# A second buffer for the split probabilities (ph) in a two-layer hybrid attention / mLSTM backbone

## The chip, the cores and the metric

The kernel runs on one core of one Trainium2 chip. The metric is device time in microseconds (us) of one execution, taken as the median of several runs. One core has TensorE (PE in the profile, with its weight loads as PEld), VectorE (DVE), ScalarE (ACT), GpSimd (POOL) and SyncE (SP), which issues the DMAs. Each engine works its own instructions off in the order in which they were emitted and waits on semaphores for the others.

## The reference

A latent stream x of 2048 tokens and a context of 256 tokens, both 1024 wide, go through two layers. In each layer the normed and modulated input is projected; the columns are split into windowed attention (8 query heads, 2 key/value heads of 64) and a bidirectional mLSTM (4 heads of 128); both are gated, concatenated and projected out. Cut to what the change touches, the attention is:

```python
s_win = jnp.einsum('bnqhgd,bnkhd->bhgnqk', qb, kw) * scale      # 128 queries, 3 x 128 keys
s_ctx = jnp.einsum('bnqhgd,bchd->bhgnqc', qb, kc) * scale       # 256 context keys
s_sink = sink.reshape(1, KV, G, 1, 1, 1)                        # one logit per head
p = jax.nn.softmax(jnp.concatenate([s_win, s_ctx, s_sink], axis=-1), axis=-1)
out = einsum(p_win, vw) + einsum(p_ctx, vc)
x = x + gate_x * (jnp.concatenate([att_x * silu(az), m_x], -1) @ w_out)
```

The context rows only attend to the context, and they go through the out-projection in the first layer alone.

## The kernel before

All matrix products of float32 values are made from pairs of fp16 parts (hi, lo) in three passes, so an operand is scaled by a power of two and split before it goes to TensorE.

**Attention.** It runs in four units of two heads in a layer. A unit goes over blocks of 128 queries (18 in the first layer, 16 in the second). For a block b and each of its heads h, `score` takes one of the two 1024-wide PSUM tiles `d` and multiplies query and key pairs into it: 640 columns for an inner block (two neighbours, two context blocks, the block itself), 512 or 256 elsewhere. Its `post` task then does, in this order: VectorE adds the mask and takes the maximum; VectorE makes the bias (`smx`); ScalarE takes the exponent in place, with the row sum; ScalarE copies the result times 16384 into the left half of the fp16 tile `ph` (line 1108); VectorE writes the rest, product minus that copy, to the right half (line 1110), after which `d` is given back; SyncE issues a DMA transpose of `ph` into one of three tiles `pp` (line 1114), and when that has read it, `ph` is free again. `ph` has one buffer (line 388). Once both heads' transposes have landed, `pv` multiplies probabilities and values ("PV", `b<-vp,pp` in the profile, 20 matmuls for an inner block). Around these, `qproj` (q for two blocks, `b<-xt,wa`, 24 matmuls of 256 columns) and `zproj` (the gate, `b<-wa,xt`, 24 of 128 columns) project with the weights `wa`. There are 136 blocks in all, hence 272 scores and transposes and 136 PVs.

**mLSTM.** For each of four heads `mproj` projects q, k and v and runs the forward states, and `mmix` goes over the chunks of 128 tokens backwards: a load of decay rows (`mb<-mD`, three buffers), GpSimd and ScalarE make the decay from them, TensorE makes two transposed products (`kT`), the projections of the output gates (`b<-woz,xt`, 24 matmuls of 256 columns) and five float32 products with states and values (`b<-V,p`, `b<-V,toz`, `b<-s,mb`), and VectorE, ScalarE and GpSimd norm and gate the result, which goes to DRAM (`mixD`).

**Out-projection.** For a block, `loader` fetches its row of `mixD`, VectorE takes the maximum (`held<-g`), ScalarE and VectorE split it (`xt`), SyncE transposes the pair, and only after that issues the next block's load. TensorE then does 48 matmuls of 512 columns (`b<-xt,xt` in the second layer). It needs `w_out`, which is loaded into the room of the layer's input, once the attention and the mLSTM of a token group have both read that for the last time.

**What sets the order.** The program isn't written in the order in which it runs. The attention stream (`alpha`, weight 308), the mLSTM stream (`beta`, weight 560) and some smaller ones are generators. A planner (`Plan.run_until`) keeps an estimated clock for each engine and an estimated time at which each tile is written and read; `till` holds a generator until its operand is there by that estimate, `get` until a buffer is free by it, and the streams of like priority take turns by the share of TensorE's time that they have had. The next piece is emitted from whatever can go on. An instruction's place on its engine therefore follows from the estimates: a buffer that the planner holds to be taken moves all that stands behind it, and lets other streams go ahead. For the DMA transpose of `ph` the estimate is fixed by its size:

```python
            if name == "dma_start_transpose":
                return 0.8, 2.2 + b / 300e3
```

Nearly every instruction is emitted through one helper, so the profile shows line 179 for all of them, and work is told apart by the tiles' names.

Of the kernel before, what the change touches and what calls it, by code (L numbers as in the profile page):

```python
# [7 lines left out]
F16 = mybir.dt.float16  # L8
# [5 lines left out]
P = 128  # L14
D = 1024
# [49 lines left out]
def _span(v):  # L65
    """Name and range of the bytes of one partition (or of DRAM) that v covers."""
    dims = list(v.ap)
    size = 2 if v.dtype == F16 else 4
    off = v.offset
    if v.space != bass.MemoryType.DRAM:  # L70
        step = dims[0][0]
        off = off % step if step else off
        dims = dims[1:]
    lo = hi = off
    for st, n in dims:
        if st < 0:
            lo += st * (n - 1)
        else:
            hi += st * (n - 1)
    return v.name, lo * size, (hi + 1) * size  # L80
# [6 lines left out]
class Plan:  # L87
    """The order of emission.  Streams and tasks are generators: they yield True after a piece of work,
    a time to wait for, or None while a flag or a buffer is missing.  The engines' times are estimated."""

# [10 lines left out]

# [1 line left out]
    def _times(self, table, v):  # L103
# [76 lines left out]

# [1 line left out]
    def buffers(self, tag, pool, shape, dtype, bufs, psum=False):  # L182
# [17 lines left out]
    def take(self, tag, n, shape=None, dtype=None):  # L200
        """n buffers at once."""
        while True:
            if self.cnt[tag] + n > self.spec[tag][3]:
                yield None
            elif sorted(self.rel[tag])[n - 1] > self.now + 0.5:
                yield sorted(self.rel[tag])[n - 1]
            else:
                return [self.new(tag, shape, dtype) for _ in range(n)]
# [22 lines left out]

# [1 line left out]
    def till(self, *aps, slack=0.2):  # L233
# [74 lines left out]
class Kern(Plan):  # L308
# [33 lines left out]

# [1 line left out]
    def mm(self, out, lhsT, rhs, start=True, stop=True):  # L344
# [5 lines left out]
    def mm3(self, out, lh, rh, step=6):  # L350
        """Three passes over pairs: lh, rh give the operand of (hi or lo, k)."""
        c = 0
        yield from self.till(lh(0, 0), lh(1, KT - 1), rh(0, 0), rh(1, KT - 1))
        for k in range(KT):
            for a, b in ((0, 0), (0, 1), (1, 0)):
                self.mm(out, lh(a, k), rh(b, k), start=(k == 0 and a + b == 0), stop=(k == KT - 1 and a == 1))
                c += 1
                if c % step == 0 and c < 3 * KT:
                    yield True

# [1 line left out]
    def open(self, es):  # L362
# [7 lines left out]
        B, NTOK, NT = self.buffers, self.NTOK, self.NT  # L370
# [5 lines left out]
        w, m, x, at, c = (lambda: self.w), (lambda: self.m), (lambda: self.x), (lambda: self.at), (lambda: self.c)  # L376
# [10 lines left out]
        B("vp", at, [P, NT, 2 * HD], F16, 1)  # L387
        B("ph", at, [P, 1280], F16, 1)
        B("pp", at, [P, 10, P], F16, 3)
# [17 lines left out]

# [1 line left out]
    def consts(self):  # L409
# [29 lines left out]

# [1 line left out]
    def scale_of(self, src, n=1, s=None, inv=None):  # L441
        """s = 2^14 / 2^floor(log2 src) and 1 / s, per partition."""
        V = self.V
        t, x = self.col(n), self.col(n)
        s = self.col(n) if s is None else s
        inv = self.col(n) if inv is None else inv
        V.tensor_scalar(t, src, 1e-30, None, ALU.max)
        V.tensor_scalar(x.bitcast(I32), t.bitcast(I32), EXPBITS, EXPBITS, ALU.bitwise_and, ALU.bitwise_xor)
        V.tensor_scalar(s, x, 8192.0, None, ALU.mult)
        V.reciprocal(inv, s)  # L450
        return s, inv

    def pmax(self, am, out):
        """out = maximum over partitions of am [P, 1], on every partition."""
        yield from self.till(am)
        b = yield from self.get("b")
        self.tr(b[:, 0:P], am.to_broadcast([P, P]))
        self.V.tensor_reduce(out, b[:, 0:P], AX.X, ALU.max)
        self.put(b)
        yield True  # L460

# [1 line left out]
    def load_w(self, key, pieces, tag, scale=None, gate=(), gram=False, early=False, fast=False, space=None, into=None):  # L463
        """pieces: dram aps [D, n <= 128].  u: the product's unit.  With gram: the power of two that
        brings products of the first 128 columns under 2^15 (Cauchy-Schwarz), and u over it."""
        V, S, G, Q = self.V, self.S, self.G, self.Q
# [11 lines left out]
        am = self.held(4)  # L478
# [20 lines left out]
        for a, st in zip(pieces, stages):  # L499
            n = a.shape[1]  # L500
# [46 lines left out]

# [1 line left out]
    def ada(self, l, parts, width, tags):  # L549
        """Rows (g (1 + scale), shift, gate) of both streams to modD; the scale of xn."""  # L550
        A, Q, V = self.A, self.Q, self.V
# [73 lines left out]

# [1 line left out]
    def rstd(self, ss, scale, eps, n=1, out=None):  # L627
        """(ss * scale + eps) ^ -1/2 with one Newton step."""
        V, G = self.V, self.G
# [13 lines left out]
    def norm_pe(self, l, b, xr, free=None):  # L643
        """xr [P, D] of block b, normed and modulated, to the pairs XT of layer l."""
        S, V = self.S, self.V
# [29 lines left out]
    def norm_dma(self, l, b, xr, grab):  # L675
        """norm_pe with the turn done by DMA."""
        g, o = self.grp(b)
# [15 lines left out]
    def split(self, pair, x, s):  # L693
        """x times the column s as the pair of fp16 parts."""
        yield from self.till(x, s)
        self.S.activation(pair[:, 0], x, AF.Copy, scale=s)
        yield from self.till(pair[:, 0])
        self.V.scalar_tensor_tensor(pair[:, 1], x, s, pair[:, 0], ALU.mult, ALU.subtract)
# [90 lines left out]

# [1 line left out]
    def rope(self, u, n, tok):  # L791
        """u [P, n] of latent tokens tok .. tok + n, turned in place."""
        V, G = self.V, self.G
# [12 lines left out]

# [1 line left out]
    def kphase(self, l):  # L808
# [67 lines left out]

# [1 line left out]
    def rphase(self, l):  # L878
# [106 lines left out]

# [1 line left out]
    def attention(self, l, j):  # L987
# [220 lines left out]

# [1 line left out]
    def mproj(self, l, h):  # L1210
# [172 lines left out]

# [1 line left out]
    def mmix(self, l, h):  # L1385
# [245 lines left out]
    def move_wo(self, l):  # L1631
        """The weights of the out-projection, from the room of the next layer's XT to their own."""
        yield from self.need(("alpha", l), ("mmix", l, MH - 1), ("wo", l, 3))
# [12 lines left out]

# [1 line left out]
    def outproj(self, l):  # L1648
# [59 lines left out]
        def scaled(gt, s):  # L1708
            """The gate with the units of the weights in it."""
            for n in range(4):  # L1710
# [34 lines left out]
        def grab(i):  # L1745
            """A buffer for a pair, and what gives it back: in the room of an XT, or a slot."""
            while True:
# [110 lines left out]

# [1 line left out]
    def loaders(self):  # L1860
# [49 lines left out]

# [1 line left out]
    def run(self):  # L1912
# [73 lines left out]
```

## Time and profile before

| | |
|---|---|
| median of 3 runs | 2785.13 us (2782.59 to 2791.67) |
| span of the profiled execution | 2804.1 us, 64646 instructions |
| TensorE busy | 2470.3 us (88%) |
| its weight loads | 1890.5 us (67%) |
| VectorE busy | 1850.9 us (66%) |
| ScalarE busy | 1488.1 us (53%) |
| GpSimd busy | 1515.6 us (54%) |
| mean granted TensorE clock | 0.966 |
| scores (`d<-ks,toz`) run | 197.9 to 2725.7 us |
| mLSTM products (`b<-V,toz`, float32) run | 317.3 to 2598.0 us |
| out-projection of layer 1 (`b<-xt,xt`, fp16) runs | 2611.6 to 2793.6 us |

The execution that was profiled took longer than the runs that were timed: its span is 2804.1 us, the median of the runs 2785.13 us, a ratio of 0.9932. From about 200 to 1300 us and from about 1600 to 2600 us attention and mLSTM of the first and the second layer are interleaved; between them lies the first out-projection with the next layer's norm, at the end the second out-projection. A wait in the profile is named by the engine and tile that waits and by what ended the wait; idle time of an engine that nobody waits for costs nothing.

### The profile page before, as it was taken

What the parts mean: (1) busy time and instruction counts of PE and PEld (TensorE: products, weight loads), DVE (VectorE), ACT (ScalarE), POOL (GpSimd) and SP (SyncE); (2) the same over time, 40 slices, a digit from 0 to 9 for tenths busy, and PEclk for the clock granted to TensorE, in tenths of its full rate; (3) what the DMA queues carried; (4) which work ended last, traced back from release to release, by engine and by line L of the source; (5) the groups of instructions that cost most, each with busy time, mean ns of one, the idle gap of its engine ahead of it and who ended that gap; (6) DMA issues with size and microseconds to landing.
All of it is one profiled execution on the core that took longest, in us unless ns stands there. A gap on an engine that the chain in (4) does not pass through costs nothing. (4 is left out here: it accounts for less than half of the span.)

```text
span 2804.1 us, 64646 instructions
## 1 busy us (share of the span) xinstructions
PE 2470.3 (88%) x23650; PEld 1890.5 (67%) x23650; DVE 1850.9 (66%) x4817; ACT 1488.1 (53%) x3788; POOL 1515.6 (54%) x2832
## 2 busy tenths in 40 slices
PE   6789899988999899888799888998898899988898
PEld 2766786678668776775355558867785787677443
DVE  4878566756575656567677676657666665757775
ACT  1546565556566655565222356655674566556421
POOL 1846476637654765275322563775577367637321
PEclk8899999999999999999899999999999999999999
DMA  8344663577446634578888636633663675267775
GB/s 265 116 130 107 139 137 84 102 147 142 111 93 146 134 58 120 116 140 198 220 209 199 153 79 123 134 84 88 144 114 96 110 137 102 62 123 164 186 190 163
DMA packets 822448, 376.16 MB, mean 134 GB/s; under 512 B 492537, under 2 KB 800241, under 8 KB 821105
## 3 DMA queue, kind: packets, MB, share of 16 engines
q1 hardware_dynamic: 822128, 372.02, 59.2%
q8 instruction: 186, 3.05, 0.5%
q14 instruction: 134, 1.09, 0.1%
HBM read 198.99 MB, written 57.56 MB: 91 GB/s over the span
## 5 line engine op out<-in xcount | busy, mean ns | idle before, releaser
L179 PEld LDWEIGHTS <-xt 128*128 128x128 f16 x12048 | 901.8, 99 | 246.2 <-issue 51.0
L179 PE MATMUL b<-woz,xt 128*128 128x256 f16 (+2 forms) x3840 | 490.8, 277 | 24.8 <-DVE p L179 13.4
L179 PE MATMUL b<-xt,wqk 128*128 128x512 f16 (+1 forms) x1824 | 390.8, 367 | 1.4 <-DVE held L179 1.4
L179 DVE SCALAR_TENSOR_TENSOR ph<-d,ph 128x640 f16<-128x640 f32 (+2 forms) x272 | 212.3, 781 | 133.3 <-ACT ph L179 131.8
L179 ACT ACTIVATE d<-d,smx,un 128x640 f32<-128x640 f32 (+2 forms) x272 | 223.4, 821 | 126.4 <-DVE smx L179 113.4
L179 PEld LDWEIGHTS <-wqk 128*128 128x128 f16 x1824 | 176.9, 99 | 167.0 <-issue 11.2
L179 PE MATMUL d<-ks,toz 128*128 128x256 f16 (+1 forms) x1568 | 190.8, 258 | 92.8 <-DVE ph L179 62.8
L179 POOL TENSOR_TENSOR p<-p 128x128 f32<-128x128 f32 x272 | 128.6, 475 | 254.2 <-ACT p L179 240.5
L179 PE MATMUL b<-wa,xt 128*128 128x128 f16 (+1 forms) x3336 | 250.1, 226 | 4.0 <-ACT toz L179 3.1
L179 POOL TENSOR_TENSOR held<-held,mhalf 128x1 f32<-128x1 f32 x200 | 115.9, 580 | 240.5 <-DVE held L179 234.7
L179 PEld LDWEIGHTS <-toz 128*128 128x128 f16 x1568 | 148.1, 100 | 139.8 <-issue 54.8
L179 PE MATMUL b<-wv,xt 128*128 128x128 f16 x3456 | 228.9, 220 | 11.3 <-DVE p L179 5.3
L179 ACT ACTIVATE ph<-d 128x640 f16<-128x640 f32 (+2 forms) x272 | 182.0, 669 | 93.3 <-DMA pp<-ph 91.7
L179 DVE CUSTOM_DVE_ANT_0 d<-d,mask 128x640 f32<-128x640 f32 (+1 forms) x240 | 196.0, 817 | 36.4 <-PE d L179 35.8
L179 POOL TENSOR_TENSOR g<-g,mb 128x512 f32<-128x512 f32 (+1 forms) x152 | 189.0, 1243 | 39.4 <-ACT g L179 28.0
L179 PE MATMUL b<-xt,wa 128*128 128x256 f16 x1632 | 198.2, 275 | 4.1 <-DVE toz L179 1.9
L179 POOL TENSOR_TENSOR mb<-mb,mask 128x256 f32<-128x256 f32 x136 | 100.9, 742 | 177.0 <-DMA mb<-mD 143.5
L179 POOL TENSOR_TENSOR toz<-toz,cs 128x256 f32<-128x256 f32 x160 | 125.3, 803 | 105.3 <-DMA cs<-in_rope 83.1
L179 PEld LDWEIGHTS <-wa 128*128 128x128 f16 x1696 | 163.7, 99 | 27.2 <-issue 5.5
L179 DVE TENSOR_REDUCE held<-g 128x1 f32<-128x1024 f32 x110 | 133.1, 1212 | 62.8 <-DMA g<-mixD 34.4
L179 PE MATMUL b<-xt,xt 128*128 128x512 f16 x768 | 169.9, 382 | 5.3 <-DMA xt<-xt 3.2
L179 DVE SCALAR_TENSOR_TENSOR g<-g,cw 128x512 f32<-128x512 f32 (+1 forms) x152 | 152.4, 1002 | 31.4 <-POOL g L179 28.5
(243 smaller groups left out, 5200.1 us busy)
## 6 DMA issues: line engine op xcount, KB each, us to landing
mb<-mD SPq DMA_DIRECT2D x136, 256.0 KB
g<-in_w_in SPq DMA_DIRECT2D x60, 512.0 KB
cs<-in_rope SPq DMA_DIRECT2D x80, 256.0 KB
mixD<-p SPq DMA_DIRECT2D x272, 64.0 KB
g<-mixD SPq DMA_DIRECT2D x34, 512.0 KB
g<-in_w_ada SPq DMA_DIRECT2D x32, 512.0 KB
g<-in_x SPq DMA_DIRECT2D x24, 512.0 KB
cfD<-s SPq DMA_DIRECT2D x136, 64.5 KB
```

Of the source, the lines that this page charges most:

```text
L179: fn(*a, **kw)
```

## The change

`ph` gets two buffers instead of one. A buffer takes 1280 fp16 values, 2560 bytes in each partition; the room is taken from the scratch that the builder keeps in each partition for the descriptors of GpSimd's DMAs, which is set to 1024 bytes. Nothing else in the code differs but comment lines, which are blank now.

```diff
@@ -385,7 +385,7 @@
         B("gc", m, [P, 5, 2, MH, NT], F32, 1)
         B("ks", at, [P, 2, NTOK], F16, 1)
         B("vp", at, [P, NT, 2 * HD], F16, 1)
-        B("ph", at, [P, 1280], F16, 1)
+        B("ph", at, [P, 1280], F16, 2)
         B("pp", at, [P, 10, P], F16, 3)
@@ -1969,7 +1969,7 @@
-    nc = bacc.Bacc("TRN2", target_bir_lowering=False, num_devices=1)
+    nc = bacc.Bacc("TRN2", target_bir_lowering=False, num_devices=1, dynamic_dma_scratch_size=1024)
```

The number of buffers is one of the things from which the planner works out its order, so most instructions stand in another place than before. Two places are shown. The first is ScalarE in layer 0, where attention and `mmix` are interleaved: `d,smx<-d,smx,un` is the exponent of a score, `ph<-d` the copy that follows it in the data, and the other rows belong to the mLSTM, to PV and to gates (numbers after a name count buffers). Before:

```order
L179 ACTIVATE d_10302,smx_10312<-d_10302,smx_10312,un_6864 128x640
L179 ACTIVATE toz_10293<-b_10295,hum_8913 128x256
L179 ACTIVATE p_9750<-p_9750,col2_10325 128x64 x2
L179 ACTIVATE p_10329<-b_10330,un_6864 128x128
L179 ACTIVATE p_10376<-b_10377,col2_10397 128x128
L179 ACTIVATE toz_10293<-b_10377,col2_10397 128x128
L179 ACTIVATE p_10231<-p_10231,held1_10354 128x128
L179 ACTIVATE p_10427<-b_10429,gc_2220 128x128
L179 ACTIVATE ph_10444<-d_10302 128x640
L179 ACTIVATE d_10412,smx_10312<-d_10412,smx_10312,un_6864 128x640
```

And a like stretch of the change:

```order
L179 ACTIVATE d_10652,smx_10521<-d_10652,smx_10521,un_6797 128x640
L179 ACTIVATE ph_10716<-d_10652 128x640
L179 ACTIVATE smx_10180<-smx_10180 128x2
L179 ACTIVATE p_10685<-b_10686,un_6797 128x128
L179 ACTIVATE p_10627<-p_10627,held1_10728 128x128
L179 ACTIVATE toz_10673<-b_10675,hum_8931 128x256
L179 ACTIVATE mb_10634<-mb_10634,gc_2220 128x128 x2
L179 ACTIVATE d_10735,smx_10742<-d_10735,smx_10742,un_6797 128x640
L179 ACTIVATE ph_10781<-d_10735 128x640
```

The copy into `ph` stood eight rows behind its exponent, and now stands right behind it.

The second place is SyncE at the end of layer 1, around the first loads of the out-projection (`g<-mixD`); `g<-in_w_out` are the last two loads of its weights, `mb<-mD` and `s<-cfD` the last loads of `mmix`, `mixD<-p` stores of attention and mLSTM, `xt<-xt` the transposes of the out-projection. Before:

```order
L179 DMA g_40121<-in_w_out 128x8x128
L179 DMA g_40122<-in_w_out 128x8x128
L179 DMA g_40131<-mixD_110 128x1024
L179 DMA mixD_110<-p_39843 128x128
L179 DMA_TRANSPOSE pp_40130<-ph_40074 128x10x128
L179 DMA mixD_110<-p_39973 128x128
L179 DMA mixD_110<-p_40102 128x128
L179 DMA_TRANSPOSE pp_40331<-ph_40293 128x10x128
L179 DMA cs_40381<-in_rope 128x2x256
L179 DMA_TRANSPOSE xt2_39876<-xt2_39876 128x16x128
L179 DMA g_40423<-mixD_110 128x1024
```

In the change:

```order
L179 DMA mb_40432<-mD_116 128x4x128
L179 DMA s_40434<-cfD_115 128x129
L179 DMA g_40447<-in_w_out 128x8x128
L179 DMA g_40448<-in_w_out 128x8x128
L179 DMA g_40457<-mixD_110 128x1024
L179 DMA mixD_110<-p_40257 128x128
L179 DMA mixD_110<-p_40348 128x128
L179 DMA_TRANSPOSE xt2_40378<-xt2_40378 128x16x128
L179 DMA g_40699<-mixD_110 128x1024
```

Transposes of `ph` stood among the loads of the out-projection, the last of them 63 rows behind the first load. Now the last stands 21 rows ahead of it, and the last loads of `mmix` stand between.

## The prediction

> **What bounds the kernel now.** I read the page's head first, then the stages, then the totals of the waits. The stage view has the length of each stretch, then the busy time (and count) of PE, PEld, DVE, ACT and POOL, then the granted clock and the DMA.
>
> ```profile
> span 2804.1 us, 64646 instructions
> q1 hardware_dynamic: 822128, 372.02, 59.2%
> q8 instruction: 186, 3.05, 0.5%
> q14 instruction: 134, 1.09, 0.1%
> ...
> 200.00:1300.00 1100.00, 987.63 (x10490) 818.14 (x10491) 702.08 (x2004) 657.82 (x1798) 647.85 (x1253) 0.98 0.58 120
> 1300.00:1600.00 300.00, 264.18 (x1573) 142.78 (x1573) 211.80 (x402) 90.36 (x141) 110.53 (x192) 0.95 0.82 200
> 1600.00:2600.00 1000.00, 883.38 (x9369) 733.22 (x9367) 661.87 (x1836) 607.24 (x1622) 613.32 (x1132) 0.97 0.54 112
> 2600.00:2804.00 204.00, 183.40 (x997) 88.82 (x997) 135.59 (x261) 57.16 (x103) 45.15 (x109) 0.98 0.68 179
> ```
>
> In the two stages where attention and mLSTM are mixed (rows one and three), TensorE is busy 987.63 of 1100 and 883.38 of 1000 us; of the other engines VectorE is nearest with 66%. Each engine works its instructions off in one fixed order, so the end moves by what TensorE waits. It idles 112.4 + 116.6 = 229 us there, and the clock takes (1 - 0.98) x 1100 + (1 - 0.97) x 1000 = 52 us more. Those 281 us are the stock from which a gain can come. Who causes them:
>
> ```profile
> DVE ph L179 <- ACT ph L179: 131.8, 108, 4.9
> ACT ph L179 <- DMA pp<-ph: 91.7, 83, 3.3
> PE d L179 <- DVE ph L179: 62.8, 67, 4.5
> PE b L179 <- DMA pp<-ph: 29.5, 28, 2.3
> PE d L179 <- DVE toz L179: 26.9, 12, 4.5
> ```
>
> (Waiter, what it waited for, total us, times, longest.) The largest wait of TensorE in the mix is 62.8 us: a score tile wants one of the two d banks, and its last reader, VectorE's second half of the split (ph), is late. It is late because ScalarE's first half stood 91.7 us for the transpose that still reads the one ph. One case in order of time (start, us, work, wait):
>
> ```profile
> 556.54 3.98 SPq L179 DMA_TRANSPOSE pp<-ph  x1
> 556.99 0.71 PE L179 MATMUL d<-ks,toz 128*128 128x256 f16 x6
> 558.67 0.83 DVE L179 CUSTOM_DVE_ANT_0 d<-d,mask 128x640 f32<-128x640 f32 x1
> 559.91 0.86 ACT L179 ACTIVATE d<-d,smx,un 128x640 f32<-128x640 f32 x1 [1.35 <-DVE smx L179]
> 560.69 0.19 ACT L179 ACTIVATION_READ_ACCUMULATOR d<-d,smx,un 128x1 f32 x1
> 564.47 0.70 ACT L179 ACTIVATE ph<-d 128x640 f16<-128x640 f32 x1 [3.07 <-DMA pp<-ph]
> 565.20 0.82 DVE L179 SCALAR_TENSOR_TENSOR ph<-d,ph 128x640 f16<-128x640 f32 x1 [3.42 <-ACT ph L179]
> 566.08 0.71 PE L179 MATMUL d<-ks,toz 128*128 128x256 f16 x6 [2.89 <-DVE ph L179]
> ```
>
> Score at 557, exponent done at 560.9, but the copy into ph starts at 564.47, because the transpose of the score before was issued at 556.54 and still reads ph. TensorE stops for 2.89 us at 563.2. With ph free, copy and subtraction would follow at 560.9 + 0.70 + 0.82 = 562.4, before TensorE came to the wait. A d bank would have lived 562.4 - 557.6, about 5.0 us, instead of 8.5.
>
> **The change, part by part.** The scratch: q1 is fed by SyncE alone in the list of issues, and besides it only instruction fetch has a queue, so nothing uses the scratch that is cut; price nothing. No instruction is added or removed; busy work stays as it is. What changes is the order: the planner stops holding the copy back. In the listing of ScalarE the copy stands 9.9 rows behind its exponent on average before (next to it in 21 of 272), and 1.1 rows in the change (next to it in 253).
>
> (a) The d wait, 62.8 us. It does not go to zero: the planner now also sets scores closer together. I priced TensorE's listing with the trace's own durations (matmuls of 256 columns and float32 pairs from the rows under (d), 512 columns at twice 256, the rest from these):
>
> ```profile
> 1002.22 1.01 PE L179 MATMUL b<-vp,pp 128*128 128x128 f16 x20
> ...
> 2605.09 1.50 PE L179 MATMUL b<-wa,xt 128*128 128x128 f16 x24
> ```
>
> From that I took the work between one score's end and the start of the score after next, which is what hides the life of a bank. Its median falls from 10.1 to 8.9 us. Summing what is missing to a life of 5.0 us gives 2.9 us before and 10.0 in the change; to 6.0 us, 10.7 and 28.5; to 6.5 us, 16.3 and 41.8. Lives differ, so I take 20 us left: gain 43. Bounds: 57.8 (5 left) and 21 (42 left).
>
> (b) The clock. A stop of TensorE is followed by half clock:
>
> ```profile
> 495.00:502.00 7.00, 7.00 (x70) 5.36 (x70) 6.41 (x10) 3.11 (x9) 5.89 (x9) 1.00 0.29 75
> 502.00:505.60 3.60, 0.61 (x5) 0.23 (x4) 3.37 (x9) 2.26 (x5) 2.94 (x5) 1.00 0.06 18
> 505.60:509.00 3.40, 3.40 (x13) 1.52 (x11) 3.33 (x8) 0.87 (x2) 1.53 (x3) 0.50 0.34 77
> 509.00:516.00 7.00, 7.00 (x68) 4.49 (x67) 4.14 (x13) 4.07 (x11) 0.45 (x1) 1.00 0.31 77
> ```
>
> After 2.99 us without work the clock is 0.50 for 3.4 us: 1.7 us lost. Of the 52 us lost so in the mix I give the d wait its share of the idle time, 62.8 / 229: 14 us, and of that what (a) saves, 43 / 62.8: gain 9. Bounds 0 and 14.
>
> The Trainium skill ("TensorE: Matmul & The Clock Gate", section "What's actually happening") has the throttle come back after an idle window of about 3.4 us; by it hardly any d wait (longest 4.5 us, 0.9 us on average) would cost clock, and the forecast would lie 9 us higher. The row at 502 to 509 shows it after 2.99 us, so the row decides here.
>
> (c) The PV wait, 29.5 us. PV needs both transposes. In the priced listing the work from the second score's end to its PV falls from a median of 16.1 to 11.6 us, the shortest from 8.3 to 5.0. The chain shortens too, by the 3.07 us and more of the case above, but what is left is the landing, which the planner sets at a fixed time and the case above shows drawn out (3.98 us to issue). I take 10 us more. Bounds: 15 less (half of it gone), 30 more (doubled).
>
> (d) mLSTM alone. With the attention stream faster, it ends first: after the last score, the listing has some 8 blocks of mmix alone in layer 1 and 5 in layer 0 (before: none, the last scores stand behind the last mmix in layer 1 and beside it in layer 0). TensorE needs 1007.09 - 1003.35 = 3.74 us for such a block:
>
> ```profile
> 1003.35 2.78 PE L179 MATMUL b<-woz,xt 128*128 128x256 f16 x24
> 1005.97 0.39 PE L179 MATMUL b<-V,p 128*128 128x129 f32 x2
> 1007.09 2.78 PE L179 MATMUL b<-woz,xt 128*128 128x256 f16 x24
> ...
> L179 POOL TENSOR_TENSOR mb<-mb,p 128x256 f32<-128x256 f32 x136 | 101.0, 744 | 0.0
> L179 POOL TENSOR_TENSOR mb<-mb,mask 128x256 f32<-128x256 f32 x136 | 100.9, 742 | 177.0 <-DMA mb<-mD 143.5 <-PE b L179 29.8 <-PE d L179 2.1
> L179 POOL TENSOR_SCALAR toz<-toz 128x128 f32<-128x128 f32 x136 | 41.7, 307 | 21.9 <-ACT toz L179 21.6
> L179 POOL TENSOR_TENSOR held<-held,mhalf 128x1 f32<-128x1 f32 x200 | 115.9, 580 | 240.5 <-DVE held L179 234.7 <-PE b L179 4.5 <-DVE g L179 0.8
> L179 POOL TENSOR_TENSOR p<-p,hg 128x128 f32<-128x128 f32 x136 | 63.4, 466 | 8.1 <-DVE p L179 4.8 <-DVE col L179 1.4 <-DVE held L179 0.7
> ```
>
> GpSimd has in a block 0.744 + 0.742 + 0.307 + 0.580 + four products like the last row (0.466 each) = 4.24 us, and a few one-column steps. Alone, 13 blocks run at GpSimd's pace, 0.5 us and more above TensorE's: 7 us and up. I take 10. Bounds: 0 (buffers cover it) and 55 (rival C).
>
> (e) The tail. The out-projection at the end is paced by its loader:
>
> ```profile
> L179 SPq DMA_DIRECT2D g<-mixD x16: 424/984/1787, 2590.9 to 2769.5; - x16
> ...
> 2655.56 5.03 DMA g<-mixD
> 2666.84 5.35 DMA g<-mixD
> ```
>
> Sixteen loads from 2590.9 to 2769.5 are 11.9 us each, undisturbed 2666.84 - 2655.56 = 11.3. Before, the last blocks of attention are done under this tail. Behind the first of these loads the listing before has 24.6 us of other matmuls, the change 11.2: 13.4 us of work move out from under the loader into the mix, where TensorE is the bound. Without the transposes of ph in SyncE's queue the loader gains back 15 x 0.6 = 9. Net cost 5; bounds -9 and 13.
>
> Sum: -43 - 9 + 10 + 10 + 5 = **-27 us** on 2804.1: 2777. The median of the runs, 2785.13, is 0.9932 of the profiled span; with the same ratio 2777 becomes **2758 us** (-1.0%).
>
> **The rivals.** A change below 0.3% (8 us: under 2777, over 2793) is what a measurement of this kernel can't tell from none.
>
> A, the stops only change their names. Scores and PVs come as close as the planner's too short latencies allow, the residue of (a) is 42 us, (b) gives 4, (c) costs 15, (d) 10, (e) 5: -21 - 4 + 30 = +5, near 2790. For it: the bank's cover falls below 6.5 us in 28 places, where it was 12. Against: the copy's 91.7 us wait really goes.
>
> B, everything goes: d wait down to 5, clock 14, (c) to (e) nothing: -72, 2732 x 0.9932 = 2713. Against: the listing's places above.
>
> C, slower: the mLSTM blocks left alone are served load by load.
>
> ```profile
> 2255.13 4.95 DMA mb<-mD
> ...
> 1002.16 0.69 ACT L179 ACTIVATE mb<-mb,gc 128x128 f32<-128x128 f32 x2
> ```
>
> A block then takes 4.95 + 0.742 + 0.69 + 0.744 and the steps between, some 8.0 us instead of 3.74: 13 x 4.3 = 55 us in place of (d)'s 10. If SyncE's queue is the cause, PV is late with it and (c) is at its bound of 30: -52 + 30 + 55 + 5 = +38, 2823 in the median. It decides (over 8 us slower) from 7.2 us a block with (c) as forecast, from 5.7 with (c) at its bound. For it: GpSimd stands 143.5 us for these loads. Against: three mb buffers keep three of them in flight.
>
> D, the change does nothing (the second buffer is never needed): 2785. Against: the listing moves 232 copies.
>
> **How the numbers follow.** Forecast 0.58 (its own range 2738 to 2777), A 0.20, B 0.08, C 0.12, D 0.02. Faster: 0.54 of the forecast, B, and a fifth of A: 0.66. Slower: C and a quarter of A: 0.17. Same: the rest, 0.17. The range for 8 in 10 leaves out most of B below and most of C above: 2725 to 2798.
>
> **What would show it.** In the changed profile: "ACT ph <- DMA pp<-ph" under 15 us (if not, the buffer is not the wait); "PE d <- DVE ph" 10 to 40; "PE b <- DMA pp<-ph" 25 to 55; TensorE's idle time in the mixed stages 190 to 215 in place of 229; granted clock there up by 0.005; the last PV before the last mmix; mixD loads 11.3 us apart. I am wrong if the d wait stays over 45, if the PV wait passes 70, or if the last mmix blocks of a layer take over 7 us each.

## The result, and the profile after

The changed kernel takes 2809.4 us (median of 4 runs, 2807.02 to 2812.37), the kernel before on the same chip 2784.71 us (4 runs, 2782.59 to 2791.67). The ratio is 1.0081, with a 95% interval of 1.0064 to 1.0098: the change makes the kernel 0.8% slower. The forecast was 2758 us; 2809.4 lies above its whole range.

The head of the page after, and below it TensorE's line of the page before:

```profile
span 2805.8 us, 64709 instructions
PE 2475.1 (88%) x23650; PEld 1895.9 (68%) x23650; DVE 1846.8 (66%) x4817; ACT 1504.8 (54%) x3788; POOL 1518.0 (54%) x2832
```

```profile
PE 2470.3 (88%) x23650; PEld 1890.5 (67%) x23650; DVE 1850.9 (66%) x4817; ACT 1488.1 (53%) x3788; POOL 1515.6 (54%) x2832
```

TensorE is busy 2475.1 us in place of 2470.3 and idle 2805.8 - 2475.1 = 330.7 us in place of 2804.1 - 2470.3 = 333.8. So by the profiles nothing was gained or lost, while the timed runs differ by 24.7 us. The profiled execution of the kernel before was longer than its timed runs (2804.1 us against 2791.67 at most), and the profiled execution after (2805.8) is an ordinary one of its kernel. A difference of some 10 us between two profiled executions says nothing by itself; verdicts below go by the timed runs, and the profiles are read for where the waits are.

The totals of the waits after (waiter, what it waited for, us in total, times, longest):

```profile
DVE ph L179 <- ACT ph L179: 106.8, 87, 4.4
PE b L179 <- DVE p L179: 64.2, 53, 4.7
PE b L179 <- DVE toz L179: 27.6, 18, 4.0
PE d L179 <- DVE toz L179: 18.0, 18, 2.7
PE b L179 <- DMA xt<-xt: 19.9, 12, 6.3
PE b L179 <- DVE s L179: 15.9, 18, 2.4
PE b L179 <- DMA pp<-ph: 12.4, 16, 2.1
PE d L179 <- DVE ph L179: 11.1, 10, 2.9
ACT ph L179 <- DMA pp<-ph: 5.9, 4, 3.0
```

The same view of the kernel before, for the four that the prediction did not show:

```profile
PE b L179 <- DVE p L179: 42.1, 44, 2.7
PE b L179 <- DVE toz L179: 8.3, 10, 1.9
PE b L179 <- DMA xt<-xt: 8.3, 8, 4.0
PE b L179 <- DVE s L179: 4.5, 9, 0.8
```

The buffer does what it says: ScalarE's wait for the transpose falls from 91.7 us to 5.9, the d wait from 62.8 to 11.1, the PV wait from 29.5 to 12.4. The last two are TensorE's own, and on them it waits 68.8 us less. But it waits 64.2 + 27.6 + 15.9 + 18.0 = 125.7 us for VectorE's other work (p, toz and s on the mLSTM's and the projections' PSUM tiles b, toz on d), where it was 42.1 + 8.3 + 4.5 + 26.9 = 81.8: 43.9 us more. For the transposes of the out-projection (xt) it waits 11.6 us more, and the small rest is spread over many rows: all idle time taken together fell by the 3.1 us above. And VectorE itself still stands 106.8 us in front of its half of the split, waiting for ScalarE's half (131.8 before). That wait fell by a fifth only.

One such place in order of time, after (start, us, work, wait):

```profile
390.29 0.88 ACT L179 ACTIVATE d<-d,smx,un 128x640 f32<-128x640 f32 x1
392.28 0.69 ACT L179 ACTIVATE mb<-mb,gc 128x128 f32<-128x128 f32 x2 [1.00 <-POOL mb L179]
394.51 0.70 ACT L179 ACTIVATE ph<-d 128x640 f16<-128x640 f32 x1 [0.88 <-DMA pp<-ph]
395.11 0.47 ACT L179 ACTIVATE toz<-b,hum 128x256 f32<-128x256 f32 x1
395.24 0.82 DVE L179 SCALAR_TENSOR_TENSOR ph<-d,ph 128x640 f16<-128x640 f32 x1 [4.12 <-ACT ph L179]
395.66 0.30 POOL L179 TENSOR_SCALAR toz<-toz 128x128 f32<-128x128 f32 x1 [1.79 <-ACT toz L179]
396.76 0.28 DVE L179 SCALAR_TENSOR_TENSOR p<-toz,b 128x128 f32<-128x128 f32 x1
397.10 1.23 PE L179 MATMUL b<-woz,xt 128*128 128x256 f16 x5 [1.69 <-DVE p L179]
```

ScalarE has the exponent done at 391.2, but waits 1.00 us for GpSimd's decay rows (mb) and 0.88 us for a transpose before it copies at 394.51. VectorE's next instruction is the subtraction into ph; it stands there for 4.12 us. Behind it in VectorE's fixed order, after a few short steps, is the mLSTM's product p<-toz,b, which gives a tile b back, and TensorE stops 1.69 us for that one, until 397.10. The product also needs the gate toz, which ScalarE makes behind the copy (395.11) and GpSimd finishes at 395.96; so of the stop (395.41 to 397.10) 0.55 us pass until the gate is there, 0.8 us in VectorE's queue and 0.3 us in the product. The stop carries the name of the mLSTM, and attention work standing in the queues of these two engines has a part in it. I went through all of TensorE's stops of over 1 us for p, toz or s between 200 and 2600 us: after, there are 48 (95.3 us), and in 28 of them a subtraction into ph stands in VectorE's last 4 us; in a repeated execution of the kernel before there are 25 (53.2 us), and in 5 of them it does. With a subtraction that had itself waited for ScalarE it is 12 stops (24.6 us) against 1 (1.7 us). Such a count shows what stands together, not what causes what.

The exchange of names holds for every profile of the experiments below (from the traces, behind 200 us). In the orders that the planner made for two buffers, without a further edit, TensorE's stops for VectorE are 28 to 44 us in front of scores and 134 to 147 us in front of work other than scores and PV; in the orders made for one, with one or two buffers in the pool, they are 62 to 91 and 75 to 96 us.

The end of layer 1 and the two places where mLSTM runs nearly alone, of the kernel after. The first line is from the view of a tile (shortest, median and longest issue in ns, then the first and the last start), the other two are from the view of stretches (length, then PE, PEld, DVE, ACT, POOL, granted clock, DMA):

```profile
L179 SPq DMA_DIRECT2D g<-mixD x16: 806/998/5087, 2592.3 to 2771.4; - x16
```

```profile
1285.00:1318.00 33.00, 24.79 (x227) 22.14 (x225) 21.16 (x74) 20.04 (x55) 23.65 (x59) 0.95 0.82 188
2563.00:2606.00 43.00, 37.85 (x330) 32.86 (x331) 29.29 (x99) 25.05 (x77) 34.05 (x82) 0.92 0.66 151
```

The loads of the last out-projection are (2771.4 - 2592.3) / 15 = 11.9 us apart, as before; that the transposes of ph are gone from SyncE's queue bought nothing. Where mLSTM runs nearly alone, TensorE idles 33.0 - 24.79 + 43.0 - 37.85 = 13.4 us in all. The first of the five state products marks a block; the fourth last and the last in the order of time after:

```profile
2584.84 0.39 PE L179 MATMUL b<-V,p 128*128 128x129 f32 x2
...
2597.78 0.39 PE L179 MATMUL b<-V,p 128*128 128x129 f32 x2
```

Three blocks in 12.94 us are 4.3 us each.

### The profile page after: what moved, and what is told of

It is laid out like the page before. It is cut to its first block, busy times and chain, and to the rows that moved or that the text cites. A ratio compares the mean times of both kernels' runs of the same rounds, so it can differ in the third digit from the quotient of the medians.

```text
span 2805.8 us, 64709 instructions
## 1 busy us (share of the span) xinstructions
PE 2475.1 (88%) x23650; PEld 1895.9 (68%) x23650; DVE 1846.8 (66%) x4817; ACT 1504.8 (54%) x3788; POOL 1518.0 (54%) x2832
## 5 line engine op out<-in xcount | busy, mean ns | idle before, releaser
L179 PEld LDWEIGHTS <-xt 128*128 128x128 f16 x12096 | 913.4, 100 | 316.6 <-issue 106.6
L179 PE MATMUL b<-woz,xt 128*128 128x256 f16 (+2 forms) x3856 | 502.1, 280 | 46.6 <-DVE p L179 31.7
L179 PE MATMUL b<-xt,wqk 128*128 128x512 f16 (+1 forms) x1824 | 400.6, 366 | 0.0
L179 DVE SCALAR_TENSOR_TENSOR ph<-d,ph 128x640 f16<-128x640 f32 (+2 forms) x272 | 212.1, 780 | 107.7 <-ACT ph L179 106.8
L179 PE MATMUL b<-wa,xt 128*128 128x128 f16 (+1 forms) x3344 | 264.0, 226 | 16.6 <-DVE toz L179 5.9
L179 PE MATMUL b<-wv,xt 128*128 128x128 f16 x3456 | 237.1, 220 | 9.5 <-DVE s L179 5.9
L179 PE MATMUL b<-xt,wa 128*128 128x256 f16 x1632 | 213.0, 278 | 6.6 <-DVE s L179 2.3
L179 DVE TENSOR_TENSOR toz<-toz 64x256 f16<-64x256 f32 (+2 forms) x234 | 139.3, 596 | 59.4 <-POOL toz L179 33.1
```

Of the source, the lines that this page charges most:

```text
L179: fn(*a, **kw)
```

## The experiments

The result leaves three theories. **Order:** the second buffer is worth something, but the order that the planner makes for it costs more. **Ends:** the cost is that attention runs ahead, so that mLSTM is left alone at the end of a layer. **Draw:** any new order of this program moves the time by about a per cent, and the change drew a bad one. In the expectations theory 1 is Ends, theory 2 that the stops only change their names (in the later ones: that an order made for two buffers is slower as a class, which is Order), and theory 3 is Draw. A first question is what a repeat gives.

Times are ratios to runs of the kernel before on the same chip, with 95% intervals. "Share" is the attention stream's weight in the planner (W_ALPHA, 308 in both kernels). It changes nothing but the order, so kernels of different shares are different orders of the same work. All kernels do the whole computation. The kernel before takes 2796.3 to 2797.7 us on the chips of these trials, where it took 2784.71 on that of the result, so times of different trials are compared as ratios.

**The kernel before again.** No edit.

> The kernel before once more, for a second profile of it: the profiled execution shown so far spans 2804.1 us where the timed runs have a median of 2785, while the change's profiled execution (2805.8) is as long as its runs. Expected if the first profile was an unusually slow execution: a span near 2783 us and TensorE idle some 20 us shorter in it than 324 us. Expected if profiling itself costs this kernel 20 us: again near 2804.

Measured: 0.9997 (0.9982 to 1.0013); its ten runs go from 2791.98 to 2807.62 us. A repeat gives no difference, and one execution may lie 0.5% off the median. The profiled execution spans 2800.4 us, where 2783 was expected of an ordinary one. It is among the longer of the ten (2802.26); that profiling itself adds no time is seen from the change, whose profiled executions lie below its medians.

**The buffer without the order.** The pool gets two buffers and the scratch is cut, while the planner goes on counting one. The listing of every engine is that of the kernel before.

```diff
-        tile_ = pool().tile(shape or shape0, dtype or dtype0, tag=tag, name=tag, bufs=bufs)
+        tile_ = pool().tile(shape or shape0, dtype or dtype0, tag=tag, name=tag,
+                            bufs=2 if tag == "ph" else bufs)
...
-    nc = bacc.Bacc("TRN2", target_bir_lowering=False, num_devices=1)
+    nc = bacc.Bacc("TRN2", target_bir_lowering=False, num_devices=1, dynamic_dma_scratch_size=1024)
```

> The pool has two buffers of ph and the scratch is cut, but the planner still counts one, so that every instruction stands where it stood before. This is the second buffer without the new order. Theory 1 (the buffer helps, the new order with attention ahead of the mLSTM costs): ScalarE's wait for the transpose goes from 91.7 us to under 10, TensorE's d wait from 63 to 25-45, time 0.985 to 0.995 of before. Theory 2 (the buffer is worth nothing, as TensorE's stops only change names whatever the order): the same waits go, but the time stays within 0.3%. If it is slower by 0.8% as the change was, the order is innocent and the buffer or its place in memory is the cause.

Measured: 0.9937 (0.9921 to 0.9953). The buffer is worth 0.6%, 18 us; the cut of the scratch was not timed by itself, and whatever it costs is in that figure. So the order costs 1.0081 / 0.9937 = 1.4%, and that is the whole of the result with its sign. The waits of this kernel, then of the kernel before in the repeat on the same chip:

```profile
PE d L179 <- DVE ph L179: 40.9, 44, 4.5
PE b L179 <- DMA pp<-ph: 40.5, 33, 3.9
PE b L179 <- DVE p L179: 36.8, 38, 2.7
```

```profile
ACT ph L179 <- DMA pp<-ph: 88.0, 79, 3.3
PE d L179 <- DVE ph L179: 50.7, 56, 3.3
PE b L179 <- DMA pp<-ph: 28.2, 26, 2.8
PE b L179 <- DVE p L179: 40.1, 42, 2.8
```

ScalarE's wait for the transpose is gone (no row is left), yet the d wait falls only from 50.7 to 40.9; in this order the copy still stands some ten rows behind its exponent. The waits for p stay where they were. Stretch by stretch (first layer to its out-projection, that, the second layer, the end; cut where the first and the last load of the first out-projection and the first of the second are issued), the buffer alone:

```profile
200.00:1279.80 1079.80, 973.29 (x10418) 808.49 (x10416) 695.40 (x1980) 649.30 (x1774) 638.72 (x1227) 0.98 0.58 120
1279.80:1523.50 243.70, 216.30 (x1274) 116.11 (x1274) 179.80 (x356) 76.59 (x134) 89.25 (x167) 0.94 0.88 214
1523.50:2565.10 1041.60, 923.08 (x9678) 755.61 (x9677) 692.64 (x1884) 620.12 (x1635) 634.79 (x1162) 0.98 0.55 116
2565.10:2779.50 214.40, 191.48 (x1060) 95.46 (x1057) 143.38 (x280) 61.98 (x120) 53.18 (x127) 0.97 0.69 180
```

and the change, cut at the same events:

```profile
200.00:1302.40 1102.40, 982.61 (x10440) 815.72 (x10439) 696.49 (x1993) 665.23 (x1789) 645.27 (x1229) 0.97 0.54 118
1302.40:1536.20 233.80, 212.00 (x1233) 113.91 (x1232) 176.91 (x342) 71.62 (x115) 90.52 (x165) 0.96 0.86 219
1536.20:2592.40 1056.20, 946.34 (x9884) 772.93 (x9883) 706.37 (x1935) 644.23 (x1676) 626.86 (x1153) 0.97 0.55 117
2592.40:2805.80 213.40, 182.62 (x859) 84.64 (x856) 125.11 (x229) 47.15 (x79) 55.48 (x136) 0.96 0.60 166
```

The change is 26.3 us longer in these two executions, which ran on different chips; by the ratios the order costs 1.4%, some 40 us, and the rest is not placed here. In layer 0 the two stretches add 22.6 - 9.9 = 12.7 us, with TensorE idle 119.8 us in the mix in place of 106.5. In layer 1 some 200 matmuls have moved from the end (1060 to 859) into the mix (9678 to 9884). The mix grows by 14.6 us, and the end, paced by its loader, shrinks by 1.0: 13.6 us. Read so, half of the 26.3 us is the move, and half is stops and clock in layer 0. A second profile of the change, from the trial that repeats it, gives 17.0 us in layer 0 and 13.0 in layer 1 against the same kernel.

**The kernel before with another share, one buffer.**

```diff
-W_ALPHA = 308.0
+W_ALPHA = 302.0
```

> The kernel before, one buffer, with the attention share at 302 in place of 308: a new order of no meaning, for the scatter that reordering alone brings. Theory 3 (any new order moves the time by 0.5% or more, and the change drew a bad one): off by more than 0.4% in either direction. Theories 1 and 2: within 0.3% of before, since the ends of the streams in layer 1 stand where they stood.

Measured: 1.010 (1.0075 to 1.0126). Without any change of buffers, a weight that is 2% smaller makes the kernel 1% slower. This is as much as the change costs: a new order alone has an effect of this size.

**The buffer without the order, at that share.** The edits of the last two together.

> The order of the kernel before with share 302 (which was 1.0% slower than before), but two buffers in the pool behind the planner's one. If the second buffer by itself is worth 0.6% in any order made for one, this is 0.6% under that run: 1.003 to 1.005 of before. If the gain of the buffer alone was luck of that one order: 1.010 again.

Measured: 1.0016 (1.0 to 1.0033). Against 1.010 with one buffer and the same order this is 0.8% faster. So the buffer alone, in an order made for one, is worth 0.6% and 0.8% at these two shares.

**The change with a smaller share**, where attention runs less far ahead.

```diff
-W_ALPHA = 308.0
+W_ALPHA = 285.0
```

> The change with one number more: the attention stream's share weight is 285 in place of 308, so that attention no longer ends ahead of the mLSTM (in layer 1 the last score again stands behind the last mmix product, under the out-projection). Theory 1 (the cost is the mLSTM left alone at the layers' ends and the emptier tail): most of the 25 us come back and the gain of the d wait shows, 0.985 to 1.000 of before. Theory 2 (the stops change names all along the mixed stages): still 1.004 to 1.010.

Measured: 1.0009 (0.9991 to 1.0026). That fits Ends (attention now ends behind the last mLSTM product in layer 1 and the kernel is 0.7% faster), and Draw as well. The larger share decides.

**The change again, and the change at shares 302, 314 and 296.** The first has no edit; the others set the same line to 302.0, 314.0 and 296.0.

> The change as it is, beside the kernel before on this chip, to have it against the runs of the other experiments. Both theories: 1.005 to 1.011 of before. Below 1.003 the first result was the chip's.

> The change (planner counts two) with the share at 302. Theory 2 (an order made for two buffers has its stops at VectorE's waits everywhere and is slower as a class): 1.004 to 1.012. Theory 3 (each order is a draw, of about 1% scatter, whatever the planner counts): anywhere from 0.99 to 1.015.

> The change with the share at 314, attention still further ahead. Theory 1 (the mLSTM alone at the ends is the cost): slower than the change, 1.010 to 1.016. Theory 2: as the change, 1.004 to 1.012. Theory 3: anywhere from 0.99 to 1.015.

> The change (planner counts two) with share 296: one more draw of its class (so far 1.0009, 1.0047, 1.008, 0.995 at 285, 302, 308, 314). If the class is slower than the orders made for one: 1.000 to 1.010. Whatever the time, theory 2 expects TensorE's stops for scores under 45 us, for PV under 20, and those of all other work for VectorE at 130 to 150, where orders made for one buffer have 80 to 92.

Measured: 1.008 (1.0053 to 1.0106) again; at 302 1.0047 (1.0029 to 1.0065); at 314 0.995 (0.9934 to 0.9966); at 296 1.0000 (0.9978 to 1.0023). At 314 attention is still further ahead than in the change (in TensorE's listing its last score stands 675 rows ahead of the last mLSTM product, 510 in the change), and this is the fastest of them. **Ends falls:** running ahead is not what costs. Theory 2 had 1.004 to 1.012 there and missed as well. Steps of 2% in one planner weight move the same change between 0.5% faster and 0.8% slower than before.

In this order without its loss the waits are hardly other than in the change. At share 314:

```profile
PE b L179 <- DVE p L179: 61.0, 58, 4.7
PE d L179 <- DVE ph L179: 8.9, 7, 2.4
```

So the waits that come in place of the d wait belong to all orders made for two buffers; why they go with a loss in one and with a gain in another, these rows do not show.

**The buffer without the order, at shares 296 and 314.** The two edits of above, with 296.0 and 314.0.

> Two buffers in the pool, an order made for one, share 296: one more draw of its class (so far 0.9937 and 1.0016, against 1.000 and 1.010 for the same orders with one buffer). If the class is better than the orders made for two buffers: 0.990 to 1.002. If orders are draws without regard to class: 0.990 to 1.012.

> As the run with 296, share 314. If the class is better than the orders made for two buffers: 0.990 to 1.002. If orders are draws without regard to class: 0.990 to 1.012. The d wait and the PV wait of TensorE as in the other runs of this class, about 41 and 40 us.

Measured: 0.9879 (0.9854 to 0.9905) and 0.993 (0.9908 to 0.9953). Now there are four pairs that differ in nothing but for how many buffers the planner makes its order:

| share | order for one, two in the pool | order for two (the change) | ratio |
|---|---|---|---|
| 296 | 0.9879 | 1.0000 | 1.012 |
| 302 | 1.0016 | 1.0047 | 1.003 |
| 308 | 0.9937 | 1.0081 | 1.014 |
| 314 | 0.9930 | 0.9950 | 1.002 |

The order for two is slower in each pair (at 302 and at 314 the intervals of the two ratios overlap), by 0.8% in the mean, with a spread of 0.6% between pairs. Four pairs do not pin such a mean: its 95% interval, from that spread, is about 1% to either side. That an order for two is worse as a rule is therefore likely and not shown. That an order made for one with a second buffer in the pool is faster than the kernel before is shown in three of four; at 302 it is not, being a poor order to begin with.

**Packing.** The change lets the copy follow its exponent at once, so that attention's work comes in lumps on ScalarE and VectorE. If that is what costs, an order for two buffers in which the planner holds the copy back should lose the cost. 

```diff
+                t0 = self._times(self.wr, sp)
+                while self.now < t0 + 3.0:
+                    yield t0 + 3.0
                 ph = yield from self.get("ph")
```

The copy then stands 6.8 rows behind its exponent on average (1.1 in the change, 9.9 before). At shares 308, 296, 302 and 314:

> The change, but the planner holds the copy into ph back until 3 us after it reckons the exponent done, so attention's steps on ScalarE and VectorE are no longer packed one behind the other (6.8 rows between exponent and copy, where the change has 1.1 and before had 9.9). Theory 2 (the stop goes where attention's burst on VectorE stands): stops for VectorE by other work fall from 142 us to 90-115, stops for scores rise from 32 to 50-80, the sum stays within 20 us and the time at 0.998 to 1.010. If the burst is not the cause: other work's stops stay at 130 to 150.

> The planner counts two buffers, the copy is held back by 3 us, share 296. If the packing is what costs the orders made for two, this class comes down to that of the orders made for one: its four runs average 0.992 to 0.998, this one near 0.990. If it is something else in those orders: average 1.000 to 1.004, this one near 1.000.

> As with 296, share 302. If packing is the cause: near 1.001. If not: near 1.005. In both cases other work's stops for VectorE under 120 us.

> As with 296, share 314. If packing is the cause: near 0.993. If not: near 0.996; this one alone can't tell, it is for the average.

Measured: 1.0024 (1.0006 to 1.0042), 1.0154 (1.0122 to 1.0186), 0.9989 (0.9969 to 1.0008), 1.0058 (1.004 to 1.0077). The mean is 1.0056; that of the change at the same shares is 1.0020. Expected was a mean of 0.992 to 0.998 if packing is what costs, and 1.000 to 1.004 if not; it lies above both. Holding the copy helps twice and harms twice, so **packing is not shown to be the cost**; four pairs with such a spread do not exclude that it is a part. It does move the waits, as expected, at share 308 back toward those of before:

```profile
PE b L179 <- DVE p L179: 41.2, 54, 2.2
PE d L179 <- DVE ph L179: 36.3, 35, 2.7
PE b L179 <- DMA pp<-ph: 22.9, 22, 4.2
```

The waits for p and toz shrink as the d wait and the PV wait grow. At 296 both streams of layer 1 run into the end (in TensorE's listing the last score and the last mLSTM product stand 192 rows apart), which lasts 244 us there in place of 213 to 217:

```profile
L179 SPq DMA_DIRECT2D g<-mixD x16: 372/971/1499, 2600.3 to 2808.6; - x16
```

Its loads are (2808.6 - 2600.3) / 15 = 13.9 us apart. That is about 30 of the 43 us by which this kernel is slower than the one before (2839.58 against 2796.33); the same happens, less so, in the change at share 302.

**The best version again.** Two buffers in the pool, the planner counting one, share 296, without a further edit.

> Two buffers in the pool, the order made for one, share 296, once more: 0.9879 the first time. If that was the order and not the moment: 0.984 to 0.992 again.

Measured: 0.990 (0.9872 to 0.9928), 2771.51 us against 2796.33. It is faster than the kernel before by 1.0 to 1.2% in two trials, and than the change by 1.8 to 2.0% (0.990 and 0.9879 against 1.0081). The waits of the first trial:

```profile
PE b L179 <- DVE p L179: 48.6, 43, 3.9
PE b L179 <- DMA pp<-ph: 45.5, 26, 8.2
PE d L179 <- DVE ph L179: 36.4, 37, 4.5
```

None of these is small. It wins although 36 us of the d wait stand in it, where the change has 11.

**What stays open.** What in the order costs the time is not shown. What the four pairs have in common, by the heads of their pages, is TensorE's idle time: span less busy time is longer in the order for two by 6.5 us at 308, 15.1 at 302, 7.2 at 314 and 14.6 at 296, in the mean 11 us or 0.4%, where two executions of one kernel differ by 4 to 8. Its busy time goes both ways. The move of work from under the loader into the mix does not explain the cost as a rule: fewer matmuls are left in the end in all four pairs, but mix of layer 1 and end together are longer by 13.7 us at 308, 33.5 at 302 and 2.4 at 296, and shorter by 2.3 at 314, which leaves the fewest in the end. It was not tried by itself either (an order for two that keeps the last attention blocks at the end). What decides the draw of a single order beyond that, I could not settle.

## Why the prediction was wrong

**(a) The d wait: the wait was right, the gain was not.** The row went from 62.8 to 11.1 us, below the 20 assumed; ScalarE's row came to 5.9, under 15. But the sum took each microsecond of the wait away from TensorE's time. That is the step that failed. 43.9 us of it came back as TensorE's waits for VectorE on other tiles. The working priced the d banks alone, from TensorE's listing; it did not ask what else stands in VectorE's queue once the attention work is packed, though VectorE's own 131.8 us wait for ScalarE was the first row quoted. The subtraction into ph still stands 106.8 us, and now more often shortly ahead of the products that give TensorE its next tile (28 stops of 48, where it was 5 of 25). That each such stop is the subtraction's doing is not shown; shown is that stops for other work are longer in every order for two, and shrink again when the copy is held back (at share 308 the row of p from 64.2 to 41.2 us).

**(b) The clock: nothing.** The mixed stages of the change, in the prediction's cuts:

```profile
200.00:1300.00 1100.00, 980.80 (x10424) 813.91 (x10422) 696.25 (x1991) 664.27 (x1786) 643.20 (x1223) 0.98 0.54 118
1600.00:2600.00 1000.00, 896.90 (x9573) 745.43 (x9571) 669.49 (x1879) 628.34 (x1659) 602.97 (x1121) 0.97 0.55 115
```

Granted clock was to rise by 0.005 there; it is 0.98 and 0.97, as before. TensorE's idle time was to be 190 to 215 us; it is 119.2 + 103.1 = 222.3, where it was 229. The stops that are left cost about as much clock as those before did. In the profile with the order kept TensorE is busy 2304 us behind 200 us (the sum of the four stretches shown) for 23650 matmuls in all, in the change 2324; but two profiled executions of one kernel (share 296) differ by 2466.7 - 2456.9 = 9.8 us in this, so one profile does not show that the clock came there.

**(c) The PV wait: wrong sign.** Forecast +10, and 25 to 55 us in the row; it went from 29.5 to 12.4. With the buffer in the old order it did grow (28.2 to 40.5). That in the change the earlier start of the chain outweighs the closer PV is a reading; it fits that the row is back at 22.9 when the copy is held.

**(d) mLSTM alone: right.** Ten microseconds were taken; TensorE idles 13.4 us in the two places, and the last blocks are 4.3 us apart in layer 1, 6.1 and 4.0 behind the last PV of layer 0, short of the 7 that would have marked rival C.

**(e) The end: a size off.** Work moved as foreseen: some 200 matmuls, against the buffer alone. The 9 us that the loader was to gain from a queue free of transposes did not come: 11.9 us a load before and after. Measured against the buffer alone, the term is 14.6 - 1.0 = 13.6 us in place of 5, just over its upper bound of 13, if all that the mix of layer 1 grew by is put down to the move.

**The conversion to a median** rested on one profiled execution that was longer than the timed runs. It is not where the miss comes from: -27 set on the median itself gives the same 2758.

**The rivals.** A was right in kind: the stops changed their names. It was given 0.20 and 2790 us, because it looked for them on the d banks and in PV, and they came on the tiles b. B and D are excluded by the rows, C by the blocks' pace under (d). No case held the thing that the experiments showed to be largest: a new order of this program moves the time by up to 1% by itself (1.010 for one weight in the kernel before), so a forecast for a change that reorders nearly everything needed a range of at least ±1% around any sum, that is 2730 to 2786 for this one, and a higher chance of slower; 2809.4 lies outside even so. The buffer itself was worth 0.6%, two thirds of the forecast, and the order took 1.4%.

The Trainium skill ("TensorE: Matmul & The Clock Gate", section "What's actually happening"), weighed under (b), would have left the clock unchanged. The granted clock after agrees with that result, but not with its reason: the short d waits went, and other stops came in their place. Behind 200 us the trace of the kernel before has 32 stretches at half clock, and ahead of 21 of them TensorE has no stop of 3 us or more in the last 8 us; after it is 23 of 37. So here shorter stops than the page's window cost clock too.

## What to carry to other kernels

When a buffer is added in a kernel whose order is planned or written out, time it first with the order left alone (two in the pool, one in the plan); here this separated +1.4% from -0.6%. A wait removed from the engine that bounds the kernel can come back under another name, as here behind VectorE: look at what stands next in the queue of the engine that served it. And where a small step of one scheduling weight moves the time by 1%, try several such steps with any change before judging it; the best of them here beat both kernels.

## What the runs showed that I had not expected

The spread from order alone: five listings of the change give 0.995 to 1.008, four of them with the copy held 0.999 to 1.015, and neighbouring weights (302 and 308, one buffer) differ by 1.0%. In the first trial of the buffer alone more of the gain lies in TensorE's busy time, and so in the clock, than in idle time: between the profiled executions of the kernel before in the repeat and of the buffer alone busy time falls by 2470.5 - 2455.3 = 15.2 us at the same 23650 matmuls (granted clock in the mix of layer 1 0.98, in the repeat 0.96), and idle time by 5.7, as the two heads show, before:

```profile
span 2800.4 us, 64646 instructions
PE 2470.5 (88%) x23650; PEld 1893.4 (68%) x23650; DVE 1850.4 (66%) x4817; ACT 1488.5 (53%) x3788; POOL 1513.9 (54%) x2832
```

and with the buffer alone (span 2779.5 us):

```profile
PE 2455.3 (88%) x23650; PEld 1883.0 (68%) x23650; DVE 1851.3 (67%) x4817; ACT 1483.3 (53%) x3788; POOL 1514.2 (54%) x2832
```

At share 302 it was the other way round (from the traces, 12 us idle and 5 us busy time). As busy time differs by 9.8 us between two executions of one kernel, two profiles cannot tell which of the two the buffer returns.
